# The first stage of a hybrid RWKV-7 block with its tensor-engine order written out, on one Trainium2 core

## The chip, the cores and the metric

One core of one Trainium2 chip runs the whole program once. The metric is the device time of that execution in microseconds (us), lower is better. Engines are named as the profile names them: PE is the tensor engine's matmuls and PEld its weight loads, DVE the vector engine, ACT the scalar engine, POOL GpSimd, SP the engine whose queue issues nearly all DMAs (SPq).

## What is computed

One layer: two streams of 256 tokens (context and latent), model width 2048. The first stage, the only one that the change touches, computes the shift and scale vectors from the conditioning, normalises and modulates the tokens, and makes the first 832 columns of the input projection.

```python
def rms_norm(x, g):
    xf = x.astype(jnp.float32)
    y = xf * lax.rsqrt(jnp.mean(xf * xf, axis=-1, keepdims=True) + RMS_EPS)
    return (y * g.astype(jnp.float32)).astype(x.dtype)

def adaln(cvec, w, b):
    m = jax.nn.silu(cvec) @ w + b
    return jnp.split(m[:, None, :], N_MOD, axis=-1)

def modulate(h, shift, scale):
    return h * (1.0 + scale) + shift
...
        sh1, sc1, ga1, sh2, sc2, ga2 = adaln(c, w_mod[i], b_mod[i])
        csh1, csc1, cga1, csh2, csc2, cga2 = adaln(c_ctx[None, :], w_mod[i], b_mod[i])
        px = modulate(rms_norm(x, norm_mix[i]), sh1, sc1) @ w_in[i]
        pc = modulate(rms_norm(xc, norm_mix[i]), csh1, csc1) @ w_in[i]
```

After it come the other columns of the projection, the RWKV scans in both directions, a short convolution, a Fourier mixing, the output projection and a gated feed-forward network.

## The kernel before

The model width is cut into 16 K-tiles of 128 (`KT`). The first stage is `phase_a`; its loop `for k in range(KT)` does for each K-tile k four things, which this document names as the changed code does.

- **Modulation** of k: four DMAs of 512 KB bring the modulation weights (`wm`, six buffers, so one and a half K-tiles) and 16 small float32 matmuls sum them with the conditioning into one PSUM bank, `pmod`, of which there is one. DVE copies the result out (`am`, L457).
- **Tokens** of k: two tiny matmuls turn `am` by a selection matrix into columns in the same bank; DVE adds the bias (`m4`, L461, the trace calls it m) and makes the scale (L463); ACT applies both to the normalised tokens (L468, once a stream), casts them to `XH` (L266), and DVE takes the remainder `XL` (L269). `xn`, the normalised tokens, is made by DVE (L465) ahead of time, with three buffers.
- **Weights** of k: one DMA of 416 KB (`wa`, two buffers), a DVE cast `wh` (L268) and a POOL subtraction `wl` (L269), two buffers each.
- **Products** of k: seven column blocks (`pacc0` to `pacc6`, seven PSUM banks that sum over all K-tiles), each of six matmuls: `wh` with `XH` and `XL`, `wl` with `XH`, for two streams. 42 matmuls a K-tile. All go through the helper line L233.

A scheduler with a timing model of its own decides in what order each engine gets these instructions. Each engine runs its own list in order, and a wait at the head of a list holds up what stands behind it. The list that the scheduler made for PE runs, in the middle of the stage: the products of K-tile k, then the tokens of k+1, then the modulation of k+2, then the products of k+1. Within the products it takes the first factor of all seven blocks for one stream, then for the other, and mixes the rest. On DVE the cast `wh` of k+2 stands ahead of `m4` of k+1, and the `wl` of k+2 on POOL follows that cast.

After the stage, `conv_both` and `conv3` (ACT L325, DVE L326 and L328) read the finished banks, in an order written by hand that begins with blocks 5 and 6, and `phase_kv` begins, whose first projection writes the bank that block 5 had. Its weights `w` come in tiles of 256 KB and POOL makes both halves (`whi` L268, `wlo` L269).

Of the kernel before, what the change touches and what calls it, by code (L numbers as in the profile page):

```python
# [10 lines left out]
F32 = mybir.dt.float32  # L11
F32R = mybir.dt.float32r
# [5 lines left out]
P = 128  # L18
D = 2048
KT = D // P  # L20
L = 256
# [13 lines left out]
NA = 5  # L35
WA_COLS = 192 + NA * P
# [164 lines left out]
class Builder:  # L201
# [209 lines left out]
    def phase_a(self, st):  # L411
        tc, nc, a = self.tc, self.nc, self.a
        pa = st.enter_context(tc.tile_pool(name="pa", bufs=2))
        ps = st.enter_context(tc.tile_pool(name="psA", bufs=1, space=PSUM))
        x32 = [self.t(pa, [P, 2 * L], F32, f"x32_{k}", 1) for k in range(KT)]
        for k in range(KT):
            nc.sync.dma_start(x32[k], a["xin"][:, k])
        n0 = P + 2
        nc.sync.dma_start(self.consts[:, :n0], a["consts"][:, :n0])
        nc.sync.dma_start(self.vecs, a["vecs"])  # L420

        sc = self.sc = self.t(self.cp, [P, KT, 32], F32, "sc")
        th = self.t(pa, [P, KT, 2], F32, "th", 1)
        nc.gpsimd.memset(sc, 0.0)
        nc.scalar.activation(th, self.cct, AF.Tanh, scale=0.5)
        nc.vector.scalar_tensor_tensor(th, th, 1.0, self.cct, op0=ALU.add, op1=ALU.mult)
        nc.vector.tensor_scalar_mul(sc[:, :, 0:2], th, 0.5)

        pst = self.t(ps, [P, 2 * L], F32, "pacc5")
        for k in range(KT):  # L430
            sq = self.t(pa, [P, 2 * L], F32, "xn", 3)
            if k % 2:
                nc.scalar.square(sq, x32[k])
            else:
                nc.vector.tensor_tensor(sq, x32[k], x32[k], op=ALU.mult)
            self.rms_add(pst, sq, k)
        prs = self.rms_finish(pst, pa, ps, 2 * L, "pacc6")
        rstd = self.t(pa, [P, 2 * L], F32, "rstd", 1)
        nc.vector.tensor_copy(rstd, prs)
        widths = [96, 96] + [P] * NA  # L440
        offs = np.cumsum([0] + widths)
        acc = [self.t(ps, [P, 2 * L], F32, f"pacc{b}") for b in range(2 + NA)]
        bm = self.vec("b_mod").rearrange("p (j k) -> p j k", j=6)
        for k in range(KT):
            am = self.t(pa, [P, 2 * P], F32, "am")
            pmk = self.t(ps, [P, 2 * L], F32, "pmod")
            for h in range(KT // GM):
                wm = self.t(pa, [P, GM, 2 * P], F32, "wm", 24 // GM)
                nc.sync.dma_start(wm, a["wma"][k, :, GM * h:GM * h + GM])
                for j in range(GM):  # L450
                    i = GM * h + j
                    q = i % 4
                    self.mm(pmk[32 * q:32 * q + 32, :2 * P], sc[:, i], wm[:, j], i < 4, i >= KT - 4)
            if k == 4:
                nc.sync.dma_start(self.consts[:, n0:], a["consts"][:, n0:])
                self.small_prep(pa)
            nc.vector.tensor_copy(am, pmk[:, :2 * P])  # L457
            for h in range(2):
                self.mm(pmk[:, 2 * P + 2 * h:2 * P + 2 * h + 2], am[:, P * h:P * h + P], self.cst("selc"), True, True)
            m4 = self.t(pa, [P, 2, 2], F32, "m4")  # L460
            nc.vector.tensor_tensor(m4, pmk[:, 2 * P:2 * P + 4].rearrange("p (j s) -> p j s", j=2),  # L461
                                    bm[:, 0:2, k].unsqueeze(2).to_broadcast([P, 2, 2]), op=ALU.add)
            nc.vector.tensor_scalar(m4[:, 1], m4[:, 1], 1.0, self.vec("norm_mix", k), op0=ALU.add, op1=ALU.mult)  # L463
            xn = self.t(pa, [P, 2 * L], F32, "xn", 3)
            nc.vector.tensor_tensor(xn, x32[k], rstd, op=ALU.mult)  # L465
            for s in range(2):
                sl = slice(s * L, s * L + L)
                nc.scalar.activation(xn[:, sl], xn[:, sl], AF.Identity, bias=m4[:, 0, s:s + 1], scale=m4[:, 1, s:s + 1])  # L468
                self.split(self.XH[s][:, k], self.XL[s][:, k], xn[:, sl], nc.scalar, nc.vector)
            wa = self.t(pa, [P, WA_COLS], F32, "wa", 2)  # L470
            nc.sync.dma_start(wa, a["wia"][k])
            wh = self.t(pa, [P, WA_COLS], F32R, "wh", 2)
            wl = self.t(pa, [P, WA_COLS], F32R, "wl", 2)
            self.split(wh, wl, wa, nc.vector, nc.gpsimd)
            for b in (*range(5, 2 + NA), *range(5)):
                c0, c1 = offs[b], offs[b + 1]
                self.mm6(acc[b][:c1 - c0], wh[:, c0:c1], wl[:, c0:c1], k)

        with tc.manual_schedule(engines={mybir.EngineType.Activation, mybir.EngineType.DVE}):
            for j in (*range(3, NA), -2, -1, *range(3)):  # L480
                if j >= 0:
                    self.conv_both(self.kctx[j], self.klat[:, j], acc[2 + j], 8 + j)
                else:
                    dst, sh = ((self.wdT, "sh_wd"), (self.adT, "sh_ad"))[j]
                    self.conv3(dst[:96], acc[2 + j][:96], self.vec(sh, 0, 3, 96), 2, L)
        nc.scalar.activation(self.wdT[:96], self.wdT[:96], AF.Tanh)
        self.dump("wdT", self.wdT)
        self.dump("adT", self.adT)
# [732 lines left out]
```

## Time and profile before

| | |
|---|---|
| median of three runs | 1837.65 us (1833.49 to 1838.82) |
| the profiled execution, its own time | 1833.69 us |
| its span in the trace | 1831.9 us |
| first product matmul of K-tile 1 in the trace | 41.47 us |
| first matmul of the next stage (tile pj) | 174.86 us |
| PE busy share over the whole span | 93% |

The trace views used here are: the page's strip of 40 equal slices of the span; tables of busy time by stretch; the timeline, which lists instructions in order of time with the idle time before each one and what ended it in brackets; and the list of waits, which sums that idle time by who waited for whom. Times are from the start of the span. A float32 matmul is recorded twice, so 16 modulation matmuls show as x32.

### The profile page before, as it was taken

Reading aid. Unit: us, or ns where it says so; the run is one execution under the profiler, and the core shown is the slowest. Engines: PE = TensorE matmul, PEld = TensorE weight load, DVE = VectorE, ACT = ScalarE, POOL = GpSimd, SP = SyncE. Lnnn points to the kernel's source line nnn. Section 1 sums busy time; section 2 is a strip of 40 time slices with the busy share of each in tenths; the row PEclk is TensorE's granted clock in tenths of the full one; section 3 lists DMA queues with packets and bytes.
Section 4 is the critical chain, followed back from the end, with each engine's and each line's share of the span. In section 5 each row is a group of like instructions: output and inputs, shape, how many; then the busy total and the mean of one; then the engine's idle time right before and its main releaser. Section 6 shows DMA issues by size and latency. Waiting matters only on the chain.

```text
span 1831.9 us, 47450 instructions
## 1 busy us (share of the span) xinstructions
PE 1702.9 (93%) x19960; PEld 1566.8 (86%) x19960; DVE 1068.0 (58%) x1851; ACT 827.7 (45%) x1577; POOL 744.5 (41%) x650
## 2 busy tenths in 40 slices
PE   7888999998899989889988889999999999999997
PEld 4767898887788878777877778999999999999996
DVE  4445247776768787768776587655555534333333
ACT  2113355565666555545553354444444444444442
POOL 1223454455666664545553453232322232333332
PEclk9999999999999999999999889999999999999998
DMA  8874224354545454344443227777777556555654
GB/s 330 313 269 159 76 79 131 122 170 136 167 149 164 140 151 132 116 151 140 144 132 92 78 93 256 243 238 242 230 231 240 191 191 198 183 189 182 191 188 137
DMA packets 139237, 318.92 MB, mean 174 GB/s; under 512 B 14224, under 2 KB 40464, under 8 KB 139024
## 3 DMA queue, kind: packets, MB, share of 16 engines
q1 hardware_dynamic: 137936, 314.84, 53.7%
q8 instruction: 156, 2.56, 0.6%
q10 hardware_dynamic: 1088, 1.05, 0.2%
q14 instruction: 57, 0.47, 0.1%
HBM read 313.74 MB, written 2.10 MB: 172 GB/s over the span
## 4 chain that ended last, share of the span: by engine, by line
PE 72%; DVE 14%; ACT 5%; issue 4%; POOL 1%; DMA 0%; DVEq 0%; ACTq 0%; POOLq 0%
PE gu L233 25%; PE pj L233 17%; PE dn L233 13%; PE iv L233 4%; PE pp L233 4%; PE st L233 3%; PE acc L233 3%; DVE macc L1070 2%; PE pacc L233 1%; DVE m L463 1%; DVE im L720 1%; DVE XL L1158 1%; DVE bk L619 1%; ACT xn L468 1%; DVE HL L1129 1%
## 5 line engine op out<-in xcount | busy, mean ns | idle before, releaser
L269 POOL TENSOR_TENSOR wlo<-w,whi 128x512 fp32r<-128x512 f32 (+2 forms) x309 | 515.4, 1671 | 750.2 <-ACT whi L266 722.9
L266 ACT CAST whi<-w 128x1024 fp32r<-128x1024 f32 (+2 forms) x472 | 401.2, 851 | 554.8 <-PE gu L233 179.9
L233 PE MATMUL gu<-XH,whi 128*128 128x256 f32 (+1 forms) x1408 | 393.0, 279 | 4.4 <-ACT whi L266 3.9
L233 PE MATMUL gu<-XH,wlo 128*128 128x256 f32 (+1 forms) x1408 | 391.4, 279 | 2.1 <-POOL wlo L269 1.3
L269 DVE TENSOR_TENSOR wlo<-w,whi 128x1024 fp32r<-128x1024 f32 (+1 forms) x175 | 206.3, 1179 | 312.6 <-ACT whi L266 312.2
L233 PE MATMUL gu<-XL,whi 128*128 128x256 f32 x1344 | 372.7, 278 | 0.1
L233 PE MATMUL pj<-XH,whi 128*128 128x256 f32 x1016 | 290.9, 315 | 3.3 <-DVE XL L1002 1.6
L233 PEld LDWEIGHTS gu<-XH,whi 128*128 128x128 f32 x1408 | 266.1, 189 | 5.7 <-ACT whi L266 4.7
L233 PEld LDWEIGHTS gu<-XH,wlo 128*128 128x128 f32 x1408 | 265.6, 189 | 2.8 <-POOL wlo L269 1.7
L233 PE MATMUL pj<-XL,whi 128*128 128x256 f32 x1016 | 260.0, 284 | 0.6 <-DVE XL L269 0.6
L233 PE MATMUL pj<-XH,wlo 128*128 128x256 f32 x1016 | 259.8, 284 | 0.0
L233 PEld LDWEIGHTS gu<-XL,whi 128*128 128x128 f32 x1344 | 253.9, 189 | 0.3 <-DVE XL L1158 0.3
L233 PEld LDWEIGHTS pj<-XH,whi 128*128 128x128 f32 x1016 | 183.7, 193 | 18.6 <-issue 3.2
L233 PE MATMUL dn<-HL,whi 128*128 128x256 f32 x704 | 196.0, 278 | 0.0
L233 PE MATMUL dn<-HH,wlo 128*128 128x256 f32 x704 | 194.4, 276 | 0.0
L233 PE MATMUL dn<-HH,whi 128*128 128x256 f32 x704 | 194.4, 276 | 0.0
L233 PEld LDWEIGHTS pj<-XL,whi 128*128 128x128 f32 x1016 | 184.4, 194 | 2.4 <-issue 0.9
L233 PEld LDWEIGHTS pj<-XH,wlo 128*128 128x128 f32 x1016 | 183.5, 193 | 2.6 <-POOL whi L268 1.7
L1070 DVE SCALAR_TENSOR_TENSOR macc<-wm,sc,macc 128x512 f32<-128x512 f32 x180 | 163.9, 910 | 1.9 <-DMA wm<-wmb 1.1
L233 PEld LDWEIGHTS dn<-HL,whi 128*128 128x128 f32 x704 | 132.1, 188 | 1.4
L233 PEld LDWEIGHTS dn<-HH,wlo 128*128 128x128 f32 x704 | 132.2, 188 | 0.0
L233 PEld LDWEIGHTS dn<-HH,whi 128*128 128x128 f32 x704 | 132.2, 188 | 0.0
(302 smaller groups left out, 2769.3 us busy)
## 6 DMA issues: line engine op xcount, KB each, us to landing
w<-wgu SPq DMA_DIRECT2D x176, 512.0 KB, 4.6
wm<-wmb SPq DMA_DIRECT2D x192, 256.0 KB, 3.1
w<-wdn SPq DMA_DIRECT2D x80, 512.0 KB, 4.5
w<-wib SPq DMA_DIRECT2D x148, 256.0 KB, 3.4
wm<-wma SPq DMA_DIRECT2D x64, 512.0 KB, 6.8
XH<-wmb SPq DMA_DIRECT2D x64, 256.0 KB, 4.6
w<-wout SPq DMA_DIRECT2D x48, 256.0 KB, 3.0
wa<-wia SPq DMA_DIRECT2D x16, 416.0 KB, 7.2
```

The source lines that it names most:

```text
L233: self.last = self.nc.tensor.matmul(out, lhsT=lhsT, rhs=rhs, start=start, stop=stop)
L266: he.copy(hi, src)
L269: le.tensor_tensor(lo, src, hi.bitcast(F32), op=ALU.subtract)
L463: nc.vector.tensor_scalar(m4[:, 1], m4[:, 1], 1.0, self.vec("norm_mix", k), op0=ALU.add, op1=ALU.mult)
L468: nc.scalar.activation(xn[:, sl], xn[:, sl], AF.Identity, bias=m4[:, 0, s:s + 1], scale=m4[:, 1, s:s + 1])
L619: V.tensor_tensor(bk[:, :, i], ch(f), ch(pi), op=ALU.mult)
L720: (G, V)[h].tensor_tensor(im[HV[h]], ga[h][HV[h]], self.bc4(cst("i64", rows=HV[h])), op=ALU.add)
L1070: V.scalar_tensor_tensor(acc, w, self.sc[:, k, 1:2], acc, op0=ALU.mult, op1=ALU.add)
L1129: V.scalar_tensor_tensor(ul[:, k, :L], X1[:, k], self.mod[:, 2, k:k + 1], uh[:, k, :L].bitcast(F32), op0=ALU.mult, op1=ALU.subtract)
L1158: V.scalar_tensor_tensor(XL[:, k], xn, bias, XH[:, k].bitcast(F32), op0=ALU.add, op1=ALU.subtract)
```

## The change

The body of the loop is cut into four functions, `modulation`, `tokens`, `weights` and `products`, and PE gets the order in which they are written (`manual_schedule` for PE alone; the other engines' lists are still the scheduler's). The products of a K-tile are cut in three pieces: blocks 5 and 6, then 0 and 1, then 2, 3 and 4. Between the first two pieces of K-tile k stand the tokens of k+1, between the last two the modulation of k+2. Within a block its six matmuls now stand together. The number of instructions on every engine is the same, and so are all sizes and buffers.

```diff
-        for k in range(KT):
-            am = self.t(pa, [P, 2 * P], F32, "am")
-            pmk = self.t(ps, [P, 2 * L], F32, "pmod")
+        ams, hls = {}, {}
+
+        def modulation(k):
+
+            ams[k] = am, pmk = self.t(pa, [P, 2 * P], F32, "am"), self.t(ps, [P, 2 * L], F32, "pmod")
             for h in range(KT // GM):
...
             nc.vector.tensor_copy(am, pmk[:, :2 * P])
+
+        def tokens(k):
+
+            am, pmk = ams.pop(k)
             for h in range(2):
...
                 self.split(self.XH[s][:, k], self.XL[s][:, k], xn[:, sl], nc.scalar, nc.vector)
+
+        def weights(k):
             wa = self.t(pa, [P, WA_COLS], F32, "wa", 2)
             nc.sync.dma_start(wa, a["wia"][k])
-            wh = self.t(pa, [P, WA_COLS], F32R, "wh", 2)
-            wl = self.t(pa, [P, WA_COLS], F32R, "wl", 2)
+            hls[k] = wh, wl = [self.t(pa, [P, WA_COLS], F32R, n, 2) for n in ("wh", "wl")]
             self.split(wh, wl, wa, nc.vector, nc.gpsimd)
-            for b in (*range(5, 2 + NA), *range(5)):
+
+        def products(k, bs):
+            wh, wl = hls[k]
+            for b in bs:
                 c0, c1 = offs[b], offs[b + 1]
                 self.mm6(acc[b][:c1 - c0], wh[:, c0:c1], wl[:, c0:c1], k)
+
+
+        with tc.manual_schedule(engines={mybir.EngineType.PE}):
+            modulation(0)
+            tokens(0)
+            weights(0)
+            modulation(1)
+            for k in range(KT):
+                products(k, (5, 6))
+                if k + 1 < KT:
+                    tokens(k + 1)
+                    weights(k + 1)
+                products(k, (0, 1))
+                if k + 2 < KT:
+                    modulation(k + 2)
+                products(k, (2, 3, 4))
```

On PE before, at the seam between the products of K-tile 1 and those of K-tile 2 (pacc are products, pmod from am the tokens, pmod from wm the modulation; a row with x4 is a quarter of a modulation):

```order
L233 MATMUL pacc_62_243<-XH_4_62,wl_377 128x256
L233 MATMUL pacc_62_243<-XH_5_63,wl_377 128x256
L233 MATMUL pmod_423<-consts_60,am_422 128x2 x2
L233 MATMUL pmod_511<-wm_512,sc_121 32x256 x4
L233 MATMUL pmod_511<-wm_518,sc_121 32x256 x4
L233 MATMUL pmod_511<-wm_524,sc_121 32x256 x4
L233 MATMUL pmod_511<-wm_530,sc_121 32x256 x4
L233 MATMUL pacc_63_244<-XH_4_62,wh_464 128x256
L233 MATMUL pacc_64_245<-XH_4_62,wh_464 128x256
```

The tokens of K-tile 2, the modulation of K-tile 3 and the products of K-tile 2 stand directly behind one another. On PE now, inside the products of K-tile 1 (weights wh_348 and wl_349), first the place behind blocks 5 and 6:

```order
L233 MATMUL pacc_64_245<-XH_4_62,wl_349 128x256
L233 MATMUL pacc_64_245<-XH_5_63,wl_349 128x256
L233 MATMUL pmod_365<-consts_60,am_364 128x2 x2
L233 MATMUL pacc_58_239<-XH_4_62,wh_348 96x256
L233 MATMUL pacc_58_239<-XH_5_63,wh_348 96x256
```

Here the tokens of K-tile 2 (am_364) have come forward by 30 products and a modulation. Then the place behind blocks 0 and 1 of the same K-tile:

```order
L233 MATMUL pacc_59_240<-XH_4_62,wl_349 96x256
L233 MATMUL pacc_59_240<-XH_5_63,wl_349 96x256
L233 MATMUL pmod_453<-wm_454,sc_121 32x256 x4
L233 MATMUL pmod_453<-wm_460,sc_121 32x256 x4
L233 MATMUL pmod_453<-wm_466,sc_121 32x256 x4
L233 MATMUL pmod_453<-wm_472,sc_121 32x256 x4
L233 MATMUL pacc_60_241<-XH_4_62,wh_348 128x256
L233 MATMUL pacc_60_241<-XH_5_63,wh_348 128x256
```

The modulation of K-tile 3 now stands between 24 and 18 products of K-tile 1. At the head of the stage all four quarters of the modulation of K-tile 1 now stand ahead of the first product, where before two of them stood behind the products of K-tile 0:

```order
L233 MATMUL pmod_249<-consts_60,am_248 128x2 x2
L233 MATMUL pmod_295<-wm_296,sc_121 32x256 x4
L233 MATMUL pmod_295<-wm_302,sc_121 32x256 x4
L233 MATMUL pmod_295<-wm_308,sc_121 32x256 x4
L233 MATMUL pmod_295<-wm_314,sc_121 32x256 x4
L233 MATMUL pacc_63_244<-XH_4_62,wh_290 128x256
```

On the other engines little moved. On DVE now, in the middle of the stage, `wh` stands ahead of `m` of the same K-tile, no longer of the one before:

```order
L459 COPY am_828<-pmod_829 128x256
L268 CAST wh_900<-wa_898 128x832
L467 TENSOR_TENSOR m_156_887<-pmod_829,vecs_59 128x4
L469 TENSOR_SCALAR m_156_887<-m_156_887,vecs_59 128x2
L269 TENSOR_TENSOR XL_6_64<-xn_890,XH_4_62 128x256
L269 TENSOR_TENSOR XL_7_65<-xn_890,XH_5_63 128x256
L471 TENSOR_TENSOR xn_1066<-x_9_28_96,rstd_237 128x512
```

So the cast of K-tile 7 (wh_900) and the scale of K-tile 7 (from pmod_829) follow each other, as they would on all later K-tiles. The lists of ACT and POOL are the same as before from beginning to end. SP's list differs in a few places, by one or two places each, and from the first weight tile of the next stage on every engine's list is the same as before.

## Rows read from the trace of the kernel before

**Rows 1.** The page's strip: granted clock and DMA share, tenths in 40 slices.

```profile
PEclk9999999999999999999999889999999999999998
DMA  8874224354545454344443227777777556555654
```

**Rows 2.** Busy time by stretch: first product of K-tile 1 to last product.

```profile
core 0: us, PE busy (x) PEld busy (x) DVE busy (x) ACT busy (x) POOL busy (x), PEclk, DMA share, GB/s
41.47:173.63 132.16, 108.60 (x1106) 94.44 (x1102) 59.10 (x99) 24.73 (x60) 32.82 (x22) 1.00 0.76 266
```

**Rows 3.** Timeline of PE, one K-tile: start, duration, instruction, idle before and releaser.

```profile
142.29 1.93 PE L233 MATMUL pacc<-XH,wh 128*128 128x256 f32 x14 [1.52 <-ACT XH L266]
...
147.39 0.50 PE L233 MATMUL pmod<-consts,am 128*128 128x2 f32 x4
148.15 1.93 PE L233 MATMUL pmod<-wm,sc 128*32 128x256 f32 x32 [0.26 <-DVE m L461]
...
151.60 1.94 PE L233 MATMUL pacc<-XH,wh 128*128 128x256 f32 x14 [1.52 <-ACT XH L266]
```

**Rows 4.** PE's waits from 41.47 to 175: us in total, times, longest.

```profile
PE pacc L233 <- ACT XH L266: 20.3, 13, 1.9
PE pmod L233 <- DVE m L461: 3.3, 13, 0.3
PE pj L233 <- DVE klat L328: 1.1, 1, 1.1
```

**Rows 5.** Timeline, the same K-tile: from the tokens' matmuls to XL.

```profile
148.13 2.00 DVE L463 TENSOR_SCALAR m<-m,vecs 128x2 f32<-128x2 f32 x1
148.13 1.97 POOL L269 TENSOR_TENSOR wl<-wa,wh 128x832 fp32r<-128x832 f32 x1 [7.34 <-DVE m L461]
...
150.16 1.09 ACT L468 ACTIVATE xn<-xn,m 128x256 f32<-128x256 f32 x2 [7.62 <-DVE m L463]
...
151.58 0.76 DVE L269 TENSOR_TENSOR XL<-xn,XH 128x256 fp32r<-128x256 f32 x2 [1.45 <-ACT XH L266]
```

**Rows 6.** Timeline of DVE, the last K-tile, with POOL idle.

```profile
166.79 0.23 DVE L463 TENSOR_SCALAR m<-m,vecs 128x2 f32<-128x2 f32 x1
```

**Rows 7.** Timeline of PE at the head of the stage.

```profile
27.61 1.93 PE L233 MATMUL pmod<-wm,sc 128*32 128x256 f32 x16 [0.26 <-DVE m L461]
30.02 3.35 PE L233 MATMUL pacc<-XH,wh 128*128 128x256 f32 x14 [0.47 <-ACT XH L266]
...
37.13 1.07 PE L233 MATMUL pmod<-wm,sc 128*32 128x256 f32 x16
38.75 0.61 PE L233 MATMUL pmod<-consts,am 128*128 128x2 f32 x4 [0.55 <-DVE am L457]
```

**Rows 8.** Issue of two wm DMAs between 20 and 22: count, KB, us to landing.

```profile
wm<-wma SPq DMA_DIRECT2D x2, 512.0 KB, 9.6
```

**Rows 9.** Busy time by stretch (columns as in rows 2): clock and DMA.

```profile
32.00:34.00 2.00, 2.00 (x11) 2.00 (x11) 1.36 (x6) 0.00 (x0) 0.00 (x0) 0.50 1.04 413
60.00:80.00 20.00, 16.46 (x171) 14.29 (x170) 9.29 (x15) 3.39 (x8) 6.23 (x3) 1.00 0.88 311
80.00:100.00 20.00, 16.46 (x170) 14.30 (x169) 8.74 (x14) 3.38 (x8) 3.92 (x2) 1.00 0.75 259
```

**Rows 10.** Tile wm from 60 to 150: the DMAs' time to landing.

```profile
DMA to landing us min/median/max: 3.9/5.8/8.8
```

**Rows 11.** Timeline around the end of the stage.

```profile
160.95 1.89 DVE L269 TENSOR_TENSOR XL<-xn,XH 128x256 fp32r<-128x256 f32 x2 [1.45 <-ACT XH L266]
161.10 4.14 POOL L269 TENSOR_TENSOR wlo<-w,whi 128x512 fp32r<-128x512 f32 x3
...
168.50 1.93 PE L233 MATMUL pacc<-XH,wh 128*128 128x256 f32 x14 [1.94 <-ACT XH L266]
...
171.67 0.47 ACT L325 ACTIVATE mq<-pacc,vecs 128x256 f32<-128x256 f32 x1 [2.92 <-PE pacc L233]
...
174.86 0.47 PE L233 MATMUL pj<-XH,whi 128*128 128x256 f32 x2 [1.09 <-DVE klat L328]
```

## The prediction

> **What bounds the kernel now.** I read the strip first, to see whether the first stage runs at the full clock and whether DMA is its limit. The three slices that lie in it have DMA at 8, 8 and 7 tenths, more than any later one but a few, and the clock at 9 tenths or more [rows 1]: DMA is used, not full. The table of the stage then says what PE does: from the first product of K-tile 1 (41.47) to the last product (173.63) it is busy 108.60 of 132.16 us at clock 1.00, with DMA at 0.76 [rows 2]. The 23.56 us that are left are what an order can win there, since work and clock are full.
>
> The timeline of one K-tile shows where they lie [rows 3]. Products run from 142.29 to 147.39, 5.10 us for 42 matmuls; the tokens take 0.50; then 0.26 of waiting for DVE; the modulation takes 1.93; then 1.52 of waiting for ACT's XH; and the next products begin at 151.60. Sum 9.31 us, the distance of the two starts. PE stops because tokens, modulation and products stand directly behind one another: XH of the next K-tile is made from the tokens that PE has just finished, and the modulation (1.93) is all that covers that chain. The list of waits says that this holds in the whole stage: 13 waits for XH, 20.3 us, 13 for m, 3.3, and one of 1.1 for the bank that the next stage writes [rows 4]. Sum 24.7.
>
> **The chain that PE waits for.** The scale (L463) takes 2.00 us where POOL's wl runs beside it for 1.97, and it ends as wl does [rows 5]; with POOL idle it takes 0.23 [rows 6]. ACT's two steps start at 150.16, XL ends at 152.34 [rows 5]. From the end of the tokens (147.89) that is 4.45 us, or 2.7 without POOL beside it.
>
> The Trainium skill's page "SBUF — State Buffer", section "SBUF: two separate sides", has a rule for this: DVE and GpSimd share a port pair, whoever starts first holds it for its whole instruction, and the other blocks fully. Rows 5 and 6 agree: 2.00 beside 0.23. By that rule nothing in the change frees the scale, since wh stands directly ahead of it on DVE now as well.
>
> **The change, part by part.** No instruction is added or removed, so PE's 108.60 us of work stay; what moves is the cover.
>
> *Tokens of k+1 come after 12 of 42 products.* Behind them on PE now stand 30 products (5.10 x 30/42 = 3.64) and the modulation (1.93), 5.57 us, before the next K-tile's products want XH. The chain needs 4.45 at its longest. Cover is left by 1.1 us, so the 20.3 us of waits for XH go.
>
> *Modulation of k+2 comes after 12 more products* (1.46 us). It wants pmod free, which m gives 0.26 us after the tokens [rows 3]. The 3.3 go too.
>
> *Tokens wait for am*, whose modulation now ends 18 + 12 products earlier, 3.6 us; uncovered, directly behind a modulation, am cost PE 0.55 [rows 7]. Nothing.
>
> *wh of k+1* needs the buffer of k-1, free when the last product of k-1 ends, so it starts as the products of k do; wl follows, 1.97 [rows 5], done under 3 us into a K-tile of over 7. Nothing, but m, the scale and XL stand behind wh on DVE: a late wa would hold all three, and with them PE.
>
> *DMA.* SP issues a wm only when the quarter of the modulation six before is done, and in order. The third quarter of the next K-tile is issued after the first quarter of this one and wanted one K-tile and a quarter later, some 8 us; landing takes 5.8 at the median and 8.8 at most [rows 10]. So 0 on most tiles, 0.8 on the worst.
>
> *Seams.* Tokens to products and modulation to products without a wait between do not occur in the trace. Products to tokens has no gap; tokens to modulation has 0.26 and a reason for it [rows 3]. There are 27 new seams; between 0 and 0.26 each that is 0 to 7.0 us. I take 0.04 each, 1.0, since the matmuls around a seam depend on nothing late and the gapless row is the nearer one.
>
> *Head of the stage.* All of the modulation of K-tile 1 stands ahead of the first product. Its second half needs two wm issued at 20.15 and 21.43 that take 9.6 to land [rows 8], so about 31.0; a quarter takes 0.96 at the low clock (two in 1.93) [rows 7], so products begin near 32.0 instead of 30.02. The half modulation of 1.07 that stood between the products of 0 and the tokens of 1 [rows 7] is gone there, and so are the waits around it. The clock was 0.50 from 32 to 34 [rows 9], behind a stretch in which PE had only modulations and waits [rows 7]. If it rises when it did, products of K-tile 1 begin near 40.8, if a few us later near 42.5; before, 41.47. I take no change, with -0.7 and +1.0 as ends.
>
> *End of the stage.* Blocks are finished one by one from the first six products of K-tile 15 on, so ACT and DVE start on block 5 at 0.8 us of that K-tile instead of 3.2 (171.67 against 168.50). Their work on it takes from 171.67 to 174.86 at the most, 3.2 us [rows 11], and is done at 4.0, inside the 5.1 of the products. The 1.1 us go. Against that, POOL's first wlo now meet XL of K-tile 15: XL took 1.89 beside wlo and 0.76 without [rows 5, 11]. Cost 0 to 1.1; I take 0.4, as XL has about a microsecond of cover.
>
> *Next stage.* POOL is done with the last wl under 3 us into K-tile 14; three wlo take 4.14 [rows 11], three whi, one-input casts, I take for no more: 11.3 at the most, of which the first pj, 10.7 after that start, needs a third. The weights are there. From there every engine's list is the same as before, so I expect the saved time to stay saved.
>
> **The sum.** From the first product of K-tile 1 to the first pj: before 174.86 - 41.47 = 133.4 [rows 3, 11]; after 108.6 + 1.0 + 0.4 = 110.0. Saved 23.4, of 24.7 us of waits. The profiled execution takes 1833.69, 4.0 under the median of the runs; there it makes 1810.3. From the median, 1837.65, it makes **1814.2 us**. A difference of under about 0.3% (5.5 us) can't be told from none.
>
> **Rivals.** *DMA becomes the bound* (12%). A K-tile brings 4 x 512 + 416 KB = 2.52 MB, and the forecast wants that in 7.57 us, 333 GB/s, where the stage now moves 266 [rows 2]. Against: 413 GB/s are there when the queue is full [rows 9], 6.1 us a K-tile. For: 60 to 80 shows 311 at a share of 0.88 [rows 9], 8.1 us. At that rate each of 13 K-tiles loses 0.54, 7.0 in all: 1821.2.
>
> The Trainium skill's page "SBUF — State Buffer", section "A bandwidth-pool intuition that's wrong (but worth ruling out)", gives some 358 GB/s from HBM to one core, an estimate of 7.05 us a K-tile from it: half a microsecond of cover instead of one and a half. The 413 of a full stretch [rows 9] is above that figure, so here the measurement decides, and the sum stays.
>
> *The order brings less than it says* (5%): a seam of a tenth or two, or the low clock staying past 38 at the head. Seams of 0.26 give 6.0 more than I took: 1820.2.
>
> *A late DMA at the head of PE's list* (2%). Before, a modulation in wait held up products that weren't ready anyway; now 18 ready products stand behind each modulation. Slower than before from the point where a K-tile takes 7.57 + 23.4/13 = 9.4 us, which is DMA at under 269 GB/s throughout. At the 259 of 80 to 100 [rows 9] a K-tile takes 9.74, 28.2 us more than forecast: 1842.4. Against it: those 259 go with a share of 0.75, so the queue waited there for buffers, not the other way round.
>
> **How the numbers follow.** Forecast as summed 81%, the rivals 12, 5 and 2. Low end: all 24.7 us go, the head wins 0.7, and the run lies 4.2 under the median as the fastest before did: 1808. High end: the DMA rival with the late clock (1821.2 + 1.0), 1822. Faster by over 0.3% in the forecast, in the DMA rival and in the seams, but for the worst of these: 95%. Within 0.3%: 3%. Slower: 2%.
>
> **What would show it.** In the profile after, products of K-tiles start 7.5 to 7.7 us apart; PE's list of waits has almost nothing for XH and m; the scale still takes 2 us or a part of it; DMA over the stage is near 330 GB/s; the first pj starts at 151 to 152 with no wait for klat. Waits of PE pmod for the DMA of wm would be the first rival, waits of products for XL or wh a late wa. Wrong altogether would be a K-tile of over 9 us, or a first pj at 151 and an end that has not moved.

## The result, and the profile after

The changed kernel takes 1811.73 us at the median of three runs (1805.89 to 1818.38), against 1837.65 before: a ratio of 0.987, 95% interval 0.984 to 0.990. A second measurement of the same two kernels, reported below, gave 1810.69 against 1838.09, 0.985 (0.981 to 0.989). Ratios further down are to runs of the kernel before that were taken together with the variant. One run of the kernel with four buffers, 1849.0, came in a slower state of the chip and is left out of its figures. The prediction was 1814.2, within 1808 to 1822.

The profiled execution takes 1805.89, its span is 1804.1, 27.8 us under that of before. The strip (clock and DMA share in tenths, 40 slices), and under it the table of the stage from the first product of K-tile 1 to the first pj (columns as in rows 2):

```profile
PEclk9999999999999999899998989999999999999998
DMA  9992233455455443544542257777777566665654
```

```profile
40.48:148.37 107.89, 107.60 (x1104) 93.23 (x1103) 47.11 (x100) 25.11 (x60) 34.53 (x23) 1.00 0.88 314
60.00:80.00 20.00, 20.00 (x210) 17.34 (x199) 10.09 (x21) 3.39 (x8) 5.99 (x4) 1.00 0.98 366
```

Where PE was busy 108.60 of 132.16 [rows 2], it is now busy 107.60 of 107.89. DMA, 0.76 of the stage before, is at 0.88, and at 0.98 from 60 to 80. The whole list of PE's waits from 40.48 to 150 is one line, where rows 4 had three and 24.7 us:

```profile
PE pacc L233 <- DVE XL L269: 0.3, 1, 0.3
```

One K-tile in the timeline (start, duration, engine, instruction), which answers to rows 3 and 5:

```profile
107.68 0.59 DVE L268 CAST wh<-wa 128x832 fp32r<-128x832 f32 x1 [1.47 <-issue]
...
108.40 1.96 POOL L269 TENSOR_TENSOR wl<-wa,wh 128x832 fp32r<-128x832 f32 x1 [5.49 <-DVE wh L268]
...
109.08 0.50 PE L233 MATMUL pmod<-consts,am 128*128 128x2 f32 x4
...
109.45 0.46 PE L233 MATMUL pacc<-XH,wh 128*96 128x256 f32 x2
109.62 0.16 DVE L467 TENSOR_TENSOR m<-pmod,vecs 128x4 f32<-128x4 f32 x1 [1.35 <-PE pmod L233]
...
109.82 0.57 DVE L469 TENSOR_SCALAR m<-m,vecs 128x2 f32<-128x2 f32 x1
...
111.01 1.93 PE L233 MATMUL pmod<-wm,sc 128*32 128x256 f32 x32
111.42 0.69 ACT L266 CAST XH<-xn 128x256 fp32r<-128x256 f32 x2
...
111.84 0.76 DVE L269 TENSOR_TENSOR XL<-xn,XH 128x256 fp32r<-128x256 f32 x2 [1.46 <-ACT XH L266]
...
112.88 0.51 PE L233 MATMUL pacc<-XH,wh 128*128 128x256 f32 x2
...
116.52 0.50 PE L233 MATMUL pmod<-consts,am 128*128 128x2 f32 x4
```

Tokens stand at 109.08 and 116.52, a K-tile of 7.44 (7.46 on the mean of the stage; before, nearly all took 9.3). XH is done at 112.11 and XL, the end of the chain, at 112.60; the products that want them begin at about 115.09. So XH, which was 1.52 late, is 3.0 early, and XL 2.5. Two things brought that, not one. The cover is longer, as the change set out. And the chain is shorter: wh now starts with the products, 1.4 us ahead of the tokens, and wl 0.7 ahead of them, so the scale beside wl takes 0.57 at this place and not 2.00 [rows 5]. Over the stage (min/median/max in ns):

```profile
L469 DVE TENSOR_SCALAR m<-m,vecs x14: 227/584/1430, 42.6 to 139.6; 128x2 f32<-128x2 f32 x14
```

At the end of the stage, XL of K-tile 15 meets wlo and costs 0.29; the first pj has no wait for klat, which rows 4 and 11 showed with 1.09:

```profile
141.69 1.90 DVE L269 TENSOR_TENSOR XL<-xn,XH 128x256 fp32r<-128x256 f32 x2 [1.46 <-ACT XH L266]
141.84 4.15 POOL L269 TENSOR_TENSOR wlo<-w,whi 128x512 fp32r<-128x512 f32 x3
...
143.64 0.39 PE L233 MATMUL pacc<-XL,wh 128*128 128x256 f32 x1 [0.29 <-DVE XL L269]
...
148.37 0.40 PE L233 MATMUL pj<-XH,whi 128*128 128x256 f32 x2
```

The first pj comes 26.5 us sooner (148.37 against 174.86). All but about 1.3 of the 27.8 us of the span are saved by then. It stays saved: the first gu by wlo of the feed-forward network starts at 1039.0 against 1066.6.

For the experiments I take the first pj as the mark of the stage. Runs of the changed kernel differ by some 13 us in all, those of the kernel before by up to 24; in two traces of the changed kernel the mark differs by 1.5, so it tells more than a single time.

### The profile page after: what moved, and what is told of

Its sections match the earlier page's. It is cut to its first block, busy times and chain, and to the rows that moved or that the text cites. A ratio compares the mean times of both kernels' runs of the same rounds, so it can differ in the third digit from the quotient of the medians.

```text
span 1804.1 us, 47455 instructions
## 1 busy us (share of the span) xinstructions
PE 1698.8 (94%) x19960; PEld 1561.3 (87%) x19960; DVE 1053.4 (58%) x1851; ACT 828.0 (46%) x1577; POOL 747.2 (41%) x650
## 4 chain that ended last, share of the span: by engine, by line
PE 77%; DVE 13%; ACT 4%; issue 3%; DMA 2%; POOL 1%; SPq 0%; DVEq 0%; ACTq 0%; POOLq 0%
PE gu L233 25%; PE pj L233 17%; PE dn L233 13%; PE pacc L233 4%; PE pp L233 4%; PE iv L233 4%; PE st L233 3%; PE acc L233 3%; DVE macc L1096 3%; PE pmod L233 2%; DVE bk L645 1%; DVE XL L1184 1%; DMA wm<-wma 1%; DVE im L746 1%; DVE HL L1155 1%
```

## The experiments

Where code is shown, the conditions on k + 1 and k + 2 are left out. The edits are to the changed kernel, but for two that are said to be to the kernel before.

### All products in one piece, and the same in the order of before

```
  products(k, (5, 6, 0, 1, 2, 3, 4))
  tokens(k + 1); weights(k + 1)
  modulation(k + 2)
```

> The changed kernel, but with all 42 products of a K-tile in one piece; tokens of k+1 and modulation of k+2 follow them. The order is still the written one, and the modulation still has its lead of two K-tiles. Theory (the gain is the work between the tokens and the next products, which covers the way tokens, scale, ACT, XH): only the modulation is left as cover, 1.93 and the 0.26 that it waits for m, against 3.71 from the end of the tokens (147.89) to the first product (151.60) in the kernel before; wh of k+2 stands ahead of m of k+1 on DVE here as before the change, so wl runs beside the scale and it takes about 2.00. So a K-tile of 9.2 to 9.4 us, waits of PE for XH of about 20 us in all and for m of about 3, the first pj near 173, and 1832 to 1838 us. Rival (the written order or the lead of the modulation brings the gain, the split into pieces nothing): a K-tile of 7.5 to 7.7, first pj at 148 to 152, about 1812 to 1815 us.

Measured: 1854.41 (1845.93 to 1860.13), ratio to before 1.008 (1.005 to 1.012); first pj at 189.19. One after the other: PE's waits from 38 to 190, the chain of one K-tile in the timeline, and the products of two K-tiles (columns as in rows 2):

```profile
PE pacc L233 <- ACT XH L266: 21.8, 14, 1.9
PE pmod L233 <- DVE m L467: 3.6, 14, 0.3
PE pacc L233 <- DVE XL L269: 1.5, 2, 1.0
```

```profile
116.51 0.59 DVE L268 CAST wh<-wa 128x832 fp32r<-128x832 f32 x1 [5.37 <-issue]
117.03 0.16 DVE L467 TENSOR_TENSOR m<-pmod,vecs 128x4 f32<-128x4 f32 x1
117.23 2.00 DVE L469 TENSOR_SCALAR m<-m,vecs 128x2 f32<-128x2 f32 x1
117.23 1.96 POOL L269 TENSOR_TENSOR wl<-wa,wh 128x832 fp32r<-128x832 f32 x1 [9.27 <-DVE m L467]
```

```profile
99.73:105.26 5.53, 5.53 (x42) 5.26 (x43) 1.68 (x4) 0.26 (x1) 0.00 (x0) 1.00 0.91 312
109.47:116.49 7.02, 7.02 (x42) 6.75 (x43) 1.67 (x4) 0.25 (x1) 0.00 (x0) 0.76 0.84 317
```

The waits are back: 1.5 for XH and 0.26 for m in each K-tile, wl and the scale starting together. So neither the written order nor the two K-tiles of lead that the modulation has bring anything; the split does. That part of the theory held. The time did not: it is slower than before, by more than I forecast. A K-tile takes 9.73 and not 9.31, since its products take 5.53 and not 5.10, and in three K-tiles the clock falls as well (0.76 in the second row, 7.02 us for the same 42 matmuls).

In the next run the products stand in the order of before; its edit, in short:

```
- for b in bs: self.mm6(acc[b], wh, wl, k)
+ for s in (0, 1): for b in bs: XH[s] by wh
+ for b in bs: XL[0] by wh
+ for b in bs: XL[1] by wh, XH[0] by wl, XH[1] by wl
```

> As the run with the tokens after all 42 products, but those products in the order of the kernel before: all 14 XH by wh first, then those with XL and wl. There a K-tile took 9.73 and not 9.31, and its products 5.53 and not 5.10. Theory: the third product of a K-tile, in the order by blocks, is one with XL, which comes 0.42 to 0.76 after XH; with the 14 XH by wh ahead XL has 1.7 us. So products of 5.1, a K-tile of 9.25 to 9.4, first pj at 173 to 182 (189.19 there), 1833 to 1845 us: what the written order has as a cost of its own, and the changed kernel covers with the rest. Rival (the 0.42 are seams of the written order, or the lower clock after a wait): a K-tile of 9.6 or more, first pj at 186 or later.

Measured: 1837.25, ratio 1.000 (0.998 to 1.002); first pj at 175.55; the products of one K-tile:

```profile
96.42:101.53 5.11, 5.11 (x42) 5.11 (x43) 1.67 (x4) 0.25 (x1) 0.00 (x0) 1.00 0.98 361
```

That is the kernel before again, to 0.7 us at the first pj. So the 0.42 belongs to the order by blocks, whose second matmul wants the XH of the other stream and whose third and fourth want XL, each as soon as it is made. The run with one piece shows it in records that are longer than usual (0.69 and 0.65 for two matmuls, where two take 0.40), not in its list of waits:

```profile
99.73 0.69 PE L233 MATMUL pacc<-XH,wh 128*128 128x256 f32 x2 [1.51 <-ACT XH L266]
100.26 0.65 PE L233 MATMUL pacc<-XL,wh 128*128 128x256 f32 x2
```

Over 14 K-tiles it makes 5.9 of the 13.6 us between the two runs; the rest goes for the most part with the pieces at the lower clock (1.5 us in each of the two K-tiles at 109 and 140, more in the last, where XL beside wlo costs another 1.0). Why the clock fell there is open: before, after like waits, it didn't. The changed kernel writes the same order by blocks and doesn't pay, because XL is 2.5 us early.

### Two pieces, and later tokens

```
  products(k, (5, 6))
  tokens(k + 1); weights(k + 1)
  products(k, (0, 1, 2, 3, 4))
  modulation(k + 2)
```

> The changed kernel, but with two pieces of products and not three: the tokens of k+1 after 12 products, then 30 products, then the modulation of k+2. Theory: the work between the tokens and the next products is the same, 3.64 + 1.93 = 5.57 us, and the scale meets wl no more than it did, so the same K-tile of 7.4 to 7.6 us, first pj at 148 to 150, no waits for XH, and a time within 5 us of 1811.7. What it tells of DMA: the wm come free 18 products, 2.2 us, later in the K-tile, for a modulation that is wanted 2.2 us later, so nothing there. Rival (the place of the modulation between the products matters, by a seam or by its wm): a K-tile above 7.8, 1817 or more, with waits of pmod for m or for the DMA of wm.

Measured: 1809.82 (1806.92 to 1816.09), ratio 0.984 (0.977 to 0.991). Most K-tiles take 7.46, first pj at 150.10. Of the 1.7 us against the changed kernel, 1.3 are there by the tokens of K-tile 5 (65.59 against 64.28), with a wait of 0.4 for XH and one of 0.3 for a wm among them; from there the distances are the same up to the last K-tile, whose XL costs 0.7 and not 0.29. So the third piece isn't needed: where the modulation stands among the products is worth nothing that can be measured.

```
  products(k, (5, 6, 0, 1, 2))
  tokens(k + 1); weights(k + 1)
  products(k, (3, 4))
  modulation(k + 2)
```

> The changed kernel, but with the tokens of k+1 after 30 of 42 products: 12 products and the modulation are left behind them, 1.46 + 1.93 = 3.4 us. Theory (the balance of cover and chain): the chain is 2.7 where wl doesn't meet the scale. wl of k+1 is done by then, so XH comes in time; but wh of k+2 now stands between the scale and XL on DVE, and its wl (1.97) starts as products of k end and meets XL, which took 1.89 beside wlo and 0.76 alone. So waits for XL of 0.3 to 1.1 us a K-tile, none for XH: a K-tile of 7.8 to 8.6 us, first pj at 153 to 164, 1816 to 1828 us. Rival (any split will do): 7.5, 148, 1812. Rival (only much cover does): 9 or more, 1832.

Measured: 1822.99 (1818.24 to 1829.29), ratio 0.992 (0.989 to 0.995); a K-tile of 8.3 to 8.6 where it waits (two K-tiles take some 7.46), first pj at 160.98. One K-tile of it in the timeline:

```profile
102.56 0.59 DVE L268 CAST wh<-wa 128x832 fp32r<-128x832 f32 x1 [0.93 <-PE pacc L233]
...
103.08 2.52 DVE L269 TENSOR_TENSOR XL<-xn,XH 128x256 fp32r<-128x256 f32 x2
103.28 2.04 POOL L269 TENSOR_TENSOR wl<-wa,wh 128x832 fp32r<-128x832 f32 x1 [6.24 <-DVE wh L268]
...
105.66 0.39 PE L233 MATMUL pacc<-XL,wh 128*128 128x256 f32 x1 [0.56 <-DVE XL L269]
```

As forecast: the cover of 3.4 us is enough for XH (but for one wait of 1.5), not for an XL that takes 2.52 beside wl and 0.76 alone [rows 5]. With 3.4 us of cover in place of 5.57 about half the gain is left (13.9 of 26.5 us at the first pj), and the wait is named XL: 6.8 us, 12 times.

### The chain shortened instead of covered

```
- nc.vector.tensor_scalar(m4[:, 1], m4[:, 1], 1.0, self.vec("norm_mix", k), op0=ALU.add, op1=ALU.mult)
+ nc.scalar.activation(m4[:, 1], m4[:, 1], AF.Identity, bias=self.vec("norm_mix", k), scale=self.vec("norm_mix", k))
```

First in the kernel before, whose order on PE stays as it was, but for a quarter of a modulation that the scheduler moved at the head:

> The kernel before, with one instruction of stage 1 on another engine: the scale of m (L463) on ACT and not on DVE, so that wl on POOL can't hold it. The order of TensorE is left as it was. Theory (PE waited for a chain that is longer than its cover, and 1.8 us of it are the scale beside wl): XH is there 1.5 to 1.8 us sooner, and of the waits for XH (20.3) 0 to 6 us are left, those for m (3.3) and klat (1.1) stay: a K-tile of 7.8 to 8.3 us, first pj at 155 to 161, 1818 to 1824 us. Rival (the waits belong to the order of PE alone, or something else stands behind the scale, such as wa or wh): a K-tile of 9.0 or more, 1832 to 1838 us.

Measured: 1820.38 (1810.13 to 1830.64), ratio 0.991 (0.987 to 0.994); a K-tile of 7.70, first pj at 155.81. The place that answers to rows 5, and the waits for XH from 41 to 157 (20.3 in rows 4):

```profile
99.90 0.39 ACT L463 ACTIVATE m<-m,vecs 128x2 f32<-128x2 f32 x1 [5.57 <-DVE m L461]
99.91 1.97 POOL L269 TENSOR_TENSOR wl<-wa,wh 128x832 fp32r<-128x832 f32 x1 [5.71 <-DVE m L461]
99.92 1.93 PE L233 MATMUL pmod<-wm,sc 128*32 128x256 f32 x32 [0.25 <-DVE m L461]
...
101.79 1.95 PE L233 MATMUL pacc<-XH,wh 128*128 128x256 f32 x14
```

```profile
PE pacc L233 <- ACT XH L266: 2.1, 1, 2.1
```

One instruction on another engine, with PE's order from K-tile 1 on untouched, brings 19.0 us at the first pj, where the change brings 26.5. Of the 19.0, 1.4 are there by the tokens of K-tile 2 (45.21 against 46.60), at the head; 17.6 come after. This is the strongest evidence for the chain: the 1.52 was the difference of a chain and its cover, and here it goes with the chain alone. That it goes with the cover alone, too, one K-tile in the run with seven buffers (further down) shows. There wl met the scale in full, in the new order:

```profile
66.38 2.02 DVE L469 TENSOR_SCALAR m<-m,vecs 128x2 f32<-128x2 f32 x1
69.86 0.76 DVE L269 TENSOR_TENSOR XL<-xn,XH 128x256 fp32r<-128x256 f32 x2 [1.46 <-ACT XH L266]
```

PE has no wait there, the products that want XL (done at 70.62) start at 71.47, and the K-tile takes 7.46. What stays in the kernel before with the scale on ACT is 0.26 for m in each K-tile and 1.1 for klat; those need the order.

The same edit in the changed kernel:

> The changed kernel with the scale of m (L469) on ACT. Theory: the chain is covered already (the last XL of a K-tile is ready about 2.5 us before its products start, 112.60 against 115.09), so a shorter chain changes nothing: a K-tile of 7.4 to 7.6, first pj within 1 us of 148.4, a time within 5 us of 1811.7. Rival (the chain still counts somewhere, at the head or at the end of the stage): first pj 1.5 us or more sooner.

Measured: 1808.05 (1804.16 to 1814.43), ratio to before 0.985 (0.982 to 0.988); a K-tile of 7.47, first pj at 150.53. Later than forecast by 1.1, and not by the chain: tokens of K-tile 2 start at 43.26 and not at 41.90, and 0.7 is lost before the products at 115.05, behind a wm that is 0.5 late. No gain from a chain that is covered; the time can't be told from that of the changed kernel.

### How much room DMA has

```
- ops = ((wh, self.XH), (wh, self.XL), (wl, self.XH))
+ ops = ((wh, self.XH), (wh, self.XL), (wl, self.XH))[:n]
...
- self.mm6(acc[b][:c1 - c0], wh[:, c0:c1], wl[:, c0:c1], k)
+ self.mm6(acc[b][:c1 - c0], wh[:, c0:c1], wl[:, c0:c1], k, n=2)
```

> The changed kernel without the third product of each block in stage 1 (wl by XH is left out, so 28 products a K-tile and not 42); wl is still made and all DMAs are the same. It measures how near the stage stands to the limit of its DMAs: PE wants 7.47 - 14 x 0.12 = 5.8 us for a K-tile, and 2.52 MB must come in that time, 434 GB/s. Theory (DMA has room in the changed kernel): a K-tile of 6.1 to 7.1 us, set by waits of pmod for the DMA of wm, at 355 to 413 GB/s; first pj at 128 to 143. Rival (the changed kernel is at the limit of DMA already, 314 to 345 GB/s): a K-tile of 7.3 or more, first pj at 146 or later.

Measured: 1789.78 in the one run, first pj at 134.10; from the tokens at 40.13 to those at 124.09, 13 K-tiles of 6.46 us:

```profile
40.13:124.09 83.96, 78.25 (x834) 60.07 (x833) 45.55 (x89) 22.01 (x52) 26.57 (x16) 1.00 1.01 390
```

With PE's work cut, the queue brings 390 GB/s over 84 us, so 6.46 a K-tile is what DMA needs and 7.47 leaves one microsecond. That settles the first rival: its 311 was what a stage asked for, not what the queue gives. The Trainium skill's page "SBUF — State Buffer", section "A bandwidth-pool intuition that's wrong (but worth ruling out)", has some 358 GB/s; the measurement is above it.

```
- wm = self.t(pa, [P, GM, 2 * P], F32, "wm", 24 // GM)
+ wm = self.t(pa, [P, GM, 2 * P], F32, "wm", 16 // GM)
```

> The changed kernel with 4 buffers for wm and not 6, so that a quarter of the modulation is fetched one K-tile ahead and not one and a half. Theory (DMA has room, but the queue is used to 0.88 of the stage): a wm is issued about 7.4 us before it is wanted and landed in 5.8 at the median before and 7.3 after; 0 to 1.5 us of wait a K-tile, a K-tile of 7.5 to 9.0, pmod waiting for the DMA of wm; first pj at 148 to 168. That would show how thin the margin is on which the new order stands: before the change such waits would have been in the shade of those for XH. Rival (buffers don't matter as long as the bytes come): a K-tile of 7.5, first pj at 148.

Measured: 1831.09 (1821.07 to 1842.57), ratio to before 0.997 (0.994 to 1.000); a K-tile of 8.29, first pj at 166.74. PE's waits from 57 to 167 and a modulation in the timeline, whose last quarter is late:

```profile
PE pmod L233 <- DMA wm<-wma: 7.1, 10, 1.4
```

```profile
109.31 1.81 PE L233 MATMUL pmod<-wm,sc 128*32 128x256 f32 x24
111.86 0.64 PE L233 MATMUL pmod<-wm,sc 128*32 128x256 f32 x8 [0.73 <-DMA wm<-wma]
```

Two buffers fewer cost most of what the change brings. And in the kernel before:

> The kernel before with 4 buffers for wm and not 6. In the changed kernel that cost 0.82 a K-tile (8.29 against 7.47), and the first pj came at 166.74 and not 148.37. Theory: it costs there because a wm is wanted 7.4 us after its issue; before the change it is wanted 9.3 after, which is more than the longest landing (8.8): a K-tile of 9.3 to 9.5, first pj at 174 to 179, within 5 us of the kernel before. So the change has used up room of the DMA queue that the kernel before had over. Rival (four buffers are too few in any order): a K-tile of 9.8 or more, first pj at 182 or later, 1842 us or more.

Measured: 1842.86, ratio 1.004 (1.003 to 1.006); first pj at 179.76, 4.9 later than before and 0.8 past what I gave. All of that is lost by the tokens at 96.48 (91.55 before), 3.6 of it by those of K-tile 2 (50.20 against 46.60); in the K-tiles from 96.48 on it takes 9.3 as it did. The scheduler also gave PE a somewhat other order in the first K-tiles of this run, so not all of the 4.9 need be the buffers'. Four buffers are too few at the head in either order, which the theory left out. With the change they cost 18.4 at the first pj: 7.5 by the tokens of K-tile 2 (49.45 against 41.90), the rest as some 0.8 in every K-tile to the last. That second part is what the order uses up. It is the reach of the buffers, not the bytes: over these K-tiles the queue brings 305 GB/s at a share of 0.88.

```
- wm = self.t(pa, [P, GM, 2 * P], F32, "wm", 24 // GM)
+ wm = self.t(pa, [P, GM, 2 * P], F32, "wm", 28 // GM)
```

> The changed kernel with 7 buffers for wm and not 6 (an eighth has no room). Theory: from the first product of K-tile 1 on there is no wait for DMA that a buffer could take away, and ahead of it the wm come as fast as the queue brings them (0.98 to 1.04 of share): a K-tile of 7.47, first pj within 1.5 us of 148.4, a time within 5 us of the changed kernel. Rival (the modulation at the head waits for buffers, not for bytes): first pj 2 us or more sooner.

Measured: 1810.98 (1808.37 to 1825.24); a K-tile of 7.47, first pj at 149.54. Six are enough.

### DVE's order written out as well, and the changed kernel again

```
- with tc.manual_schedule(engines={mybir.EngineType.PE}):
+ with tc.manual_schedule(engines={mybir.EngineType.PE, mybir.EngineType.DVE}):
```

> The changed kernel with the order of DVE written out like that of PE in stage 1. am of K-tile 0 is then ahead of xn of K-tiles 1 and 2, behind which it stood (PE waited 2.08 for it at 26.50). Theory: the head wins 0.5 to 1.5 us, the first products of K-tile 0 come at 30 to 31 and not at 31.35; xn of each K-tile (0.69) is then in the chain, 3.2 + 0.7 = 3.9 of 5.57 us of cover, so a K-tile stays at 7.47: first pj at 147 to 148, a time within 5 us of 1811.7, more likely below. Rival (DVE's own order, in which wh waits for its buffer ahead of am and m, holds the tokens): a K-tile of 7.8 or more, waits of pmod for am, 1816 us or more.

Measured: 1820.74 (1812.14 to 1825.3), first pj at 153.37: my theory missed, and the time is the rival's, though for the most part by another way. The tokens of K-tile 0 come at 24.67 and not at 26.50, yet the first products at 31.34 as against 31.35: the modulation of K-tile 1 ahead of them waits for its wm (2.5) while the queue is full (a share of 1.03 from 26 to 31), so the head is a matter of bytes. And in the middle the written order puts eleven small instructions that are due once (`small_prep`) ahead of am, one of them beside wl, and tokens wait for am (0.8):

```profile
53.43 2.11 DVE L393 TENSOR_SCALAR ab<-vecs,consts 128x8 f32<-128x8 f32 x1
...
57.11 0.42 DVE L459 COPY am<-pmod 128x256 f32<-128x256 f32 x1
...
63.34 0.59 DVE L268 CAST wh<-wa 128x832 fp32r<-128x832 f32 x1 [1.87 <-DMA wa<-wia]
```

Tokens come at 49.08, 57.58 and 67.12: two K-tiles of 8.5 and 9.5, the second by a wa that wh waits for at the head of DVE's list. In the last K-tile the products wait 1.3 for wl on POOL. DVE is better left to the scheduler here.

> The changed kernel once more, unchanged, so that it and the variants of it are told apart by more than three runs. First pj within 1 us of 148.4, since no wait but the one of 0.3 lies between 41 and there; 1806 to 1816 us. If the stage were less steady than one trace says, the first pj would move by 2 us or more.

Measured: 1810.69 (1805.27 to 1818.15), first pj at 149.87, half a microsecond outside what I gave; a K-tile of 7.47. The 1.5 us between the two traces of one kernel are there by the tokens of K-tile 2 (43.14 against 41.90) but for some 0.3.

No variant beats the changed kernel by more than these differences: with 107.60 of 107.89 us busy, PE's order has nothing left in this stage.

## Why the prediction was right

Forecast for the profiled run: first pj at 41.47 + 110.0 = 151.5, and 1810.3; measured 148.37 and 1805.89. Step by step:

- **XH, 20.3, and m, 3.3, go.** Both gone. The runs with one piece and with the scale on ACT, and the K-tile in the run with seven buffers, show that cover less chain is what decided. One sentence of this step was wrong: that nothing in the change frees the scale, because wh still stands directly ahead of m on DVE. It stands there, but it is the wh of k+1, not of k+2, and starts 1.4 us ahead of the tokens. The prediction's step on wh had the numbers for it: wl done under 3 us into a K-tile whose tokens come after 1.46. The median scale fell from 2.00 [rows 5] to 0.58. The chain was 3.0 us (109.58 to 112.60), not the 4.45 that I took as its longest, and the margin 2.5, not 1.1. The port rule of the Trainium skill's page "SBUF — State Buffer", section "SBUF: two separate sides", which the page gives for some instructions of DVE, agrees in each trace: wherever the two meet, the scale ends within 0.07 us of wl's end (110.39 and 110.36 above). Who starts first the rows don't tell; in rows 5 both starts are 148.13.
- **am, wh, wl, DMA: nothing.** Right. DMA could bring a K-tile in 6.46.
- **Seams, 1.0.** Mis-sized. Products follow the tokens after 0.37 and the modulation after 1.87, less than the 0.50 and 1.93 that those are recorded with; the products of a K-tile take 5.20 (1.56 and 3.64 above), 0.1 more than before. On balance a K-tile is 0.1 shorter than the sum of its parts, 7.53, and PE's busy time fell by 1.0 (108.60 to 107.60) where I added 1.0. A matmul's recorded tail overlaps what follows it, and where a wait stood it did not (0.50 and then 0.26 of wait [rows 3]). So seams without waits cost nothing on balance, and a wait costs a little more than the list shows. The prediction also says that modulation to products without a wait does not occur in the trace of before. It does, at 41.47 and at 58.55, each 1.86 after the modulation's start, and those rows would have given the seam:

```profile
39.61 1.93 PE L233 MATMUL pmod<-wm,sc 128*32 128x256 f32 x32 [0.26 <-DVE m L461]
41.47 1.94 PE L233 MATMUL pacc<-XH,wh 128*128 128x256 f32 x14
```

  That makes 2.0 of the 3.1 us at the first pj.
- **Head, 0 (-0.7 to +1.0).** Won 1.0 in this trace (40.48 against 41.47), but the second trace of the same kernel was 1.2 behind it by the tokens of K-tile 2, so on the two together about nothing. It goes with the clock:

```profile
27.00:31.00 4.00, 3.34 (x29) 0.98 (x33) 2.78 (x5) 1.69 (x4) 3.14 (x2) 0.57 1.03 410
31.00:35.00 4.00, 3.64 (x33) 3.07 (x26) 2.82 (x13) 0.35 (x1) 0.00 (x0) 1.00 1.03 409
```

  The granted clock, 0.57 on the mean from 27 to 31, was 1.00 from there; before the change it was still at the lower level, 0.50, from 32 to 34 [rows 9], and in the second trace of the changed kernel from 27 to 35. The 1.0 is thus luck of this trace.
- **End: klat 1.1 goes, XL of K-tile 15 costs 0.4.** Measured 0 and 0.29.
- **The next stage keeps it.** Yes: 26.5 us at the first pj, 27.6 at the first gu by wlo. The microsecond between I have not followed further, so its cause is open.
- **The rivals.** DMA as the bound: not so, by 1.0 us a K-tile. Seams: no. A late DMA at the head of PE's list: never in the stage with six buffers; but with four it is exactly what happens, and the gain shrinks to what can hardly be measured.

The 4.4 us between forecast and profiled run are thus 2.0 of seams and tails, 1.0 of the head, 0.1 of XL, and 1.3 of later stages.

## What to carry to other kernels

A repeated wait is the difference between a chain and the work that covers it: measure both, and ask which is cheaper to change. Here one instruction moved to an engine with room brought 19 us, where the new order brought 26. Before an order is tightened, measure what the DMA queue needs for the same bytes and how far ahead its buffers reach, since cover that is taken from waits is taken from the transfers too.

## What was not expected of the hardware

PE's pace has two steps at the same granted clock. Two stretches of the changed kernel, then the second of them in the run with seven buffers:

```profile
1280.00:1320.00 40.00, 40.00 (x342) 40.00 (x342) 19.81 (x23) 16.93 (x21) 12.01 (x5) 1.00 0.73 235
1400.00:1440.00 40.00, 40.00 (x355) 40.00 (x354) 19.83 (x23) 17.43 (x22) 10.12 (x6) 1.00 0.60 189
```

```profile
1400.00:1440.00 40.00, 40.00 (x343) 40.00 (x342) 18.28 (x21) 16.37 (x22) 11.56 (x5) 1.00 0.58 192
```

PE is busy throughout and the clock is 1.00, yet in 40 us it gets through 342 matmuls or 355, 4% more. The kernel before has 342 and 356 in the same stretches. In the run with seven buffers, whose first pj was like the others, the slower pace came back, and its feed-forward network took 10 us longer. A group of its matmuls in the changed kernel, then in that run (ns min/median/max, first and last start):

```profile
L233 PE MATMUL gu<-XH,wlo x1408: 276/276/542, 1039.0 to 1541.8; 128*128 128x256 f32 x168, 128*128 128x258 f32 x8
```

```profile
L233 PE MATMUL gu<-XH,wlo x1408: 276/281/549, 1040.0 to 1552.5; 128*128 128x256 f32 x168, 128*128 128x258 f32 x8
```

The median matmul is 281 ns and not 276. What sets the pace no run here shows. A difference between runs can therefore hide from the granted clock, and a mark inside the trace, at the end of the stage in question, tells more than a few runs' times.
